# Equal operand offsets for large products, a rebuilt head with its own weight buffers, and a residual that is made later, in a hybrid SSD and sparse-attention block

## The chip, the core and the metric

The kernel runs on one core of a Trainium2 chip. The metric is the device time of one launch in microseconds (us). Engines are PE (TensorE: matmuls, and its weight loads PEld), DVE (VectorE), ACT (ScalarE), POOL (GpSimd) and SP (SyncE, which issues every DMA here).

## The reference, cut to what matters

One layer on `x` of 512 tokens by 1,024 channels, in float32, with one input LayerNorm ahead of it:

```python
h = _layernorm(x, ln_in_g, ln_in_b)
mix = _mixing(h, ...)                    # below
h = _layernorm(DN_ALPHA * h + mix, ln1_g, ln1_b)
f = _conv_ffn(h, ...)                    # w_up 1024 x 5632, conv over 3 tokens, silu(a) * v, w_down 2816 x 1024
h = _layernorm(DN_ALPHA * h + f, ln2_g, ln2_b)

def _mixing(h, w_in, ...):
    proj = h @ w_in
    z, xbc, dt, q, ckv, q_idx, k_idx, w_idx, g_ssd, g_att = jnp.split(proj, ...)
    y_ssd = _ssd_branch(z, xbc, dt, ..., D_skip, ...)        # y = scan(...) + xs * D_skip[:, None]
    y_att = _dsa_branch(q, ckv, q_idx, k_idx, w_idx, ...)    # 16 heads over a latent, top-128 keys
    m = jax.nn.sigmoid(g_ssd) * (y_ssd @ w_br_ssd) + jax.nn.sigmoid(g_att) * (y_att @ w_br_att)
    return m @ w_out
```

## The kernel before

All 512 tokens are worked at once. Activations that feed a product lie with channels on the 128 partitions (`hT`, `yT`, `mT`, `h1T`, `fT`), 512 tokens along a row of 2,048 bytes. Every large product is split: an operand `a` is kept as `hi`, a copy rounded to the type `fp32r`, and `lo = a - hi`, and a product is three matmuls, hi·hi, lo·hi and hi·lo, of 512 columns each (`mm3`, `tok_mm`). A weight arrives as a 512 KB tile `wraw` (`wload`), ACT rounds it into `whi` (L173), DVE subtracts into `wlo` (L174), and SP may load the next one into a `wraw` buffer when DVE has read it (two buffers, `bufs=2`).

The stages in order: the head (load `x`, LayerNorm, transpose, split into `hhi`/`hlo`; the products of `w_small` and the first two tiles of `w_qi`); the other projections of `h`; the SSD branch (`y`, tiles `yhi`/`ylo`) with `w_br_ssd`; attention head by head (`ya`), where `tm` on POOL (L763) is the mask plus the bias of one head; `w_br_att` (`m`); `w_out`; the first DeepNorm LayerNorm (`h1`); `w_up`, convolution and gate (`f`); `w_down`; the last LayerNorm.

Two pools take SBUF from two ends. Tiles of `wraw`, `whi`, `wlo`, `hhi`, `hlo`, `h1hi`, `h1lo`, the first 15 tiles `f` and the `wo` of three `w_out` steps come from the left end; the pool `wk`, with `y`, `ya`, `m`, the other 29 tiles of `f` (`fw`, `fx`, `fy`), the `wh` of the last weights of `w_out` and `w_down`, and the queries, keys and values, lies at the right end. All these tiles are multiples of 2,048 bytes long, so all of one end start at the same place modulo 2,048: 640 at the left end, 2,016 at the right end, and 1,696 for `ckhi`/`cklo`, which stand behind a 32-byte tile `m8`. Modulo 128 this is 0, 96 and 32.

In the head, `x` token tile 1 is normalized on ACT (L292, L293) and the others on DVE (L295). `last_pow` puts POOL's subtractions of the first two `wlo` (L303) behind POOL's last power for a reciprocal root (L155). POOL then makes the residual `h` in token layout, `x·g + b`, in 16 operations (L327, L328), each on a token tile's half, and SP stores it to `htok_d` (L330). It is loaded back as `h1` (L906) when `w_out`'s last weight is loaded, and read first by DVE at L914. The vector `D` is loaded by two DMAs of single elements (L482).

The order of the instructions on each engine is found at build time by a scheduler that works from priorities; `high_priority` and `issue_after` in the code move single ones.

Of the kernel before, what the change touches and what calls it, by code (L numbers as in the profile page):

```python
# [38 lines left out]
UNITS_B = [n / 18 for n in (1, 2, 2, 5)]  # L39
NOSYNC = mybir.DependencyInfo(mybir.DependencyClass.NoSync, mybir.DependencyReason.DATA)  # L40
# [3 lines left out]
ROWS = [("dt_bias", NH), ("A_log", NH), ("idx_g", 64), ("idx_b", 64)]  # L44
# [17 lines left out]

def half_of(h):
    return slice(h * T, (h + 1) * T)
# [3 lines left out]
def block_kernel(ctx, tc, A, out):  # L68
# [6 lines left out]
    wrw = E(tc.tile_pool(name="wrw", bufs=2))  # L75
    whl = E(tc.tile_pool(name="whl", bufs=3))
    dram = E(tc.tile_pool(name="dram", bufs=1, space=DRAM))
    ps_ = E(tc.tile_pool(name="ps", bufs=1, space=PSUM))
    wk = E(tc.tile_pool(name="wk", bufs=1, side="right"))
# [22 lines left out]
    def acc_tile():  # L102
        return ps("acc", 3)
# [18 lines left out]
    for i in range(NT):  # L122
        t = wt("k4" if i < 2 else "g4", [P, D], "x")
        nc.sync.dma_start(t, A["x"][tok(i)])
        xt.append(t)
    voff, vn = _offsets(VECS)
    pvec = ct([P, vn], "pvec")
    nc.sync.dma_start(pvec, A["pvec"])
    vec = {n: pvec[:, s] for n, s in voff.items()}

    ones = ct([P, P], "ones")
# [26 lines left out]
    def split(hi, lo, src):  # L158
        nc.scalar.activation(hi, src, AF.Copy)
        nc.vector.tensor_tensor(lo, src, hi.bitcast(F32), OP.subtract)  # L160
# [115 lines left out]
    m8 = kp.tile([P, 8], F32, name="m8")  # L276
# [4 lines left out]
    dt, dts, acT, cd = [kp.tile(SH, F32, name=n, tag=n) for n in ("dt", "dts", "acT", "cd")]  # L281


    raws = [wrw.tile([P, D], F32, name="wraw", tag="wraw") for _ in range(2)]
    nc.sync.dma_start(raws[0][:, :KD * 104], A["w_small"])
    nc.sync.dma_start(raws[1], A["w_qi"][0])
    stats = [ln_stats(t, i) for i, t in enumerate(xt)]
    for i, (t, (mv, rs)) in enumerate(zip(xt, stats)):
        if i == 1:
            nm = st([P, 1], "nm")  # L290
            nc.vector.tensor_scalar(nm, mv[:, 0:1], -1.0, None, OP.mult)
            nc.scalar.activation(t, t, AF.Identity, bias=nm)  # L292
            nc.scalar.activation(t, t, AF.Copy, scale=rs)  # L293
        else:
            nc.vector.tensor_scalar(t, t, mv[:, 0:1], rs, OP.subtract, OP.mult)  # L295
    wq = []
    for j, raw in enumerate(raws):
        hi = whl.tile([P, D], F32R, name="whi", tag="whi")
        lo = whl.tile([P, D], F32R, name="wlo", tag="wlo")
        cols = slice(0, D if j else KD * 104)  # L300
        nc.scalar.activation(hi[:, cols], raw[:, cols], AF.Copy)
        with tc.issue_after(last_pow[0].ins):
            nc.gpsimd.tensor_tensor(lo[:, cols], raw[:, cols], hi[:, cols].bitcast(F32), OP.subtract)  # L303
        wq.append((hi, lo))
    wq.append(w_("w_qi", 1, ahead=0))
    accs = [acc_tile() for _ in range(3)]
    trs = ["tr", "tr", "a", "b", "c", "tr", "tr", "a"]
    for k in range(KD):
# [9 lines left out]
        split(hhi[:, k], hlo[:, k], hf)  # L318


    for j in range(2):
        gB, bB = [wt("m2", [P, T], n) for n in ("gB", "bB")]
        nc.sync.dma_start(gB, bcast(A["ln_in_g"][half_of(j)], T))
        nc.sync.dma_start(bB, bcast(A["ln_in_b"][half_of(j)], T))
        for i in range(NT):
            xh = xt[i][:, half_of(j)]
            nc.gpsimd.tensor_tensor(xh, xh, gB, OP.mult)  # L327
            nc.gpsimd.tensor_tensor(xh, xh, bB, OP.add)  # L328
            if j == 1:
                nc.sync.dma_start(htok_d[:, i], xt[i])  # L330


    hTq = [(a[:, P:], b[:, P:]) for a, b in hT]
    TQ = T - P
# [771 lines left out]
```

## Time and profile before

| | |
|---|---|
| time, median of 3 runs | 1142.55 us (1140.33 to 1143.06) |
| profiled execution | 1140.93 us, span of its instructions 1139.2 us |
| mean granted TensorE clock | 0.994 of full speed |
| PE busy | 1104.3 us, 97% of the span |
| DVE, ACT, POOL busy | 806.7, 442.8, 184.3 us |

The span reaches from the first instruction to the last; 1.7 us of the execution lie around it. PE is busy nearly all the time from 40 us on, so an engine's busy time alone says little: what counts is when PE stands still and how far apart its matmuls start. A matmul's duration in the trace includes its way through the array, and the next one starts before it ends: the distance of two starts is the price of one.

### The profile page before, as it was taken

How to read it: one execution, taken by the hardware profiler on the slowest of the kernel's cores; microseconds unless marked ns; L12 is line 12 of the kernel's file. 1: busy time of each engine (PE TensorE's matmuls, PEld its weight loads, DVE VectorE, ACT ScalarE, POOL GpSimd, SP SyncE). 2: the span in 40 equal slices, each digit the busy share in tenths (PEclk: the TensorE clock that was granted, in tenths of full speed). 3: DMA queues.
4: the chain of work that ended last, by engine and by line, in shares of the span. 5: the costliest groups of instructions: out<-in, count | busy, mean ns of one | idle time of the engine just before them, and what ended most of it. 6: DMA issues, size and time to landing. Idle time of an engine off the chain costs nothing.

```text
span 1139.2 us, 14494 instructions
## 1 busy us (share of the span) xinstructions
PE 1104.3 (97%) x5394; PEld 902.7 (79%) x5394; DVE 806.7 (71%) x1536; ACT 442.8 (39%) x694; POOL 184.3 (16%) x179
## 2 busy tenths in 40 slices
PE   4799999999999999999999999999999999999996
PEld 3688888887888888878778778889888888888885
DVE  7479798876789899958998936586665566642227
ACT  3355344434333232335645523314444444432120
POOL 7600023312113122012323300040000000000002
PEclk9899999999999999999999999999999999999999
DMA  4452133363323322322211224622223222222241
GB/s 154 149 188 87 63 140 122 126 215 112 120 102 130 130 93 75 129 97 71 88 70 66 83 84 157 225 90 74 93 94 107 96 93 93 101 103 93 93 129 74
DMA packets 43718, 125.58 MB, mean 110 GB/s; under 512 B 6801, under 2 KB 11201, under 8 KB 43649
## 3 DMA queue, kind: packets, MB, share of 16 engines
q1 hardware_dynamic: 43648, 124.67, 31.4%
q8 instruction: 42, 0.69, 0.2%
q14 instruction: 28, 0.22, 0.1%
HBM read 118.20 MB, written 9.59 MB: 112 GB/s over the span
## 4 chain that ended last, share of the span: by engine, by line
PE 73%; DVE 2%; issue 0%; DMA 0%; ACT 0%; POOL 0%; DVEq 0%; SPq 0%; ACTq 0%; POOLq 0%
PE pacc L200 42%; PE pacc L224 5%; PE pc L200 5%; PE ptr L224 4%; PE pa L200 3%; PE pb L200 3%; PE pb L224 2%; PE pc L224 2%; PE pa L224 2%; PE ptr L200 2%; PE pb L203 1%; PE pc L580 1%; PE pa L203 1%; PE pb L576 0%; DMA G<-ac_d 0%
## 5 line engine op out<-in xcount | busy, mean ns | idle before, releaser
L174 DVE TENSOR_TENSOR wlo<-wraw,whi 128x1024 fp32r<-128x1024 f32 x161 | 205.2, 1275 | 165.6 <-ACT whi L173 165.2
L173 ACT ACTIVATE whi<-wraw 128x1024 fp32r<-128x1024 f32 x161 | 170.5, 1059 | 280.9 <-PE pacc L200 163.9
L200 PE MATMUL pacc<-hhi,whi 128*128 128x512 f32 (+1 forms) x552 | 223.7, 405 | 10.7 <-ACT whi L173 10.7
L200 PE MATMUL pacc<-hlo,whi 128*128 128x512 f32 (+2 forms) x552 | 217.2, 394 | 1.4 <-DVE hlo L160 1.4
L200 PE MATMUL pacc<-hhi,wlo 128*128 128x512 f32 (+2 forms) x552 | 215.8, 392 | 0.0
L200 PEld LDWEIGHTS pacc<-hhi,whi 128*128 128x128 f32 (+1 forms) x552 | 104.2, 189 | 33.6 <-ACT whi L173 11.2
L200 PEld LDWEIGHTS pacc<-hlo,whi 128*128 128x128 f32 (+1 forms) x552 | 104.1, 189 | 24.6 <-DVE hlo L160 2.2
L200 PEld LDWEIGHTS pacc<-hhi,wlo 128*128 128x128 f32 (+1 forms) x552 | 104.0, 189 | 18.1
L155 POOL TENSOR_TENSOR rs_y<-rs_v,mhalf 128x1 f32<-128x1 f32 (+1 forms) x18 | 17.1, 954 | 504.3 <-DVE rs_v L153 501.7
L200 PE MATMUL pacc<-h1hi,wlo 128*128 128x512 f32 (+1 forms) x216 | 79.0, 366 | 0.0
L200 PE MATMUL pacc<-h1hi,whi 128*128 128x512 f32 (+1 forms) x216 | 78.9, 366 | 0.0
L200 PE MATMUL pacc<-h1lo,whi 128*128 128x512 f32 (+1 forms) x216 | 78.7, 366 | 0.0
L763 POOL TENSOR_TENSOR tm<-mask,toe 128x128 f32<-128x128 f32 (+1 forms) x64 | 45.6, 715 | 166.2 <-DVE mn L774 102.7
L585 POOL TENSOR_TENSOR v<-v,eaB 128x384 f32<-128x384 f32 x16 | 23.7, 1483 | 238.1 <-DVE eaB L583 147.1
L497 DVE SCALAR_TENSOR_TENSOR cv<-pacc,cwb,cv 128x511 f32<-128x511 f32 (+2 forms) x72 | 53.3, 741 | 0.4
L200 PE MATMUL pacc<-yhi,whi 128*128 128x512 f32 x128 | 51.8, 406 | 0.1
L200 PE MATMUL pacc<-ylo,whi 128*128 128x512 f32 x128 | 51.1, 399 | 0.0
L200 PE MATMUL pacc<-yhi,wlo 128*128 128x512 f32 x128 | 50.6, 395 | 0.0
L777 ACT ACTIVATE l<-l,mn 128x128 f32<-128x128 f32 (+1 forms) x64 | 35.7, 559 | 33.5 <-DVE mn L774 31.9
L200 PEld LDWEIGHTS pacc<-h1hi,whi 128*128 128x128 f32 x216 | 40.7, 189 | 6.7
L200 PEld LDWEIGHTS pacc<-h1hi,wlo 128*128 128x128 f32 x216 | 40.8, 189 | 6.6
L200 PEld LDWEIGHTS pacc<-h1lo,whi 128*128 128x128 f32 x216 | 40.5, 188 | 6.5
(460 smaller groups left out, 2250.7 us busy)
## 6 DMA issues: line engine op xcount, KB each, us to landing
wraw<-in_w_up_dram SPq DMA_DIRECT2D x44, 512.0 KB, 3.4
wraw<-in_w_xbc_dram SPq DMA_DIRECT2D x24, 512.0 KB, 3.5
wraw<-in_w_down_dram SPq DMA_DIRECT2D x22, 512.0 KB, 3.4
G<-ac_d SPq DMA_DIRECT2D x16, 512.0 KB, 4.4
wraw<-in_w_z_dram SPq DMA_DIRECT2D x16, 512.0 KB, 3.5
wraw<-in_w_br_ssd_dram SPq DMA_DIRECT2D x16, 512.0 KB, 3.5
eaB<-ea_d SPq DMA_DIRECT2D x32, 128.0 KB, 3.2
wraw<-in_w_ga_dram SPq DMA_DIRECT2D x8, 512.0 KB, 3.5
```

The costliest lines, as they stand in the source:

```text
L155: last_pow[0] = nc.gpsimd.tensor_tensor(y, v, mhalf[:, :n], OP.pow)
L173: nc.scalar.activation(hi[:, :cols], raw[:, :cols], AF.Copy)
L174: nc.vector.tensor_tensor(lo[:, :cols], raw[:, :cols], hi[:, :cols].bitcast(F32), OP.subtract)
L200: pe(nc.tensor.matmul(p, a, b, start=start, stop=stop).ins)
L203: pe(nc.tensor.transpose(p, a, b).ins)
L224: nc.tensor.matmul(p, x[a][:, tok(i)], w[b][h], start=first and j == 0, stop=last and j == 2)
L497: nc.vector.scalar_tensor_tensor(y[:, d:], p[:, :T - d], cwb[:, 24 * k + c:24 * k + c + 1], y[:, d:], OP.mult, OP.add)
L580: nc.tensor.matmul(yd[h * 64:(h + 1) * 64, tok(c)], xd[:, c, h], G[:, h, c], start=True, stop=True)
L585: nc.gpsimd.tensor_tensor(v[:, P:], v[:, P:], eaB[:, P:], OP.add)
L763: nc.gpsimd.tensor_tensor(tm[:, :K - f], maskt[i][:, f:], self.toe[:, 2 * P - K + f:], OP.add)
L777: nc.scalar.activation(l[:, :K], l[:, :K], AF.Exp, bias=self.mn[:, ic], scale=-1.0, accum_out=self.sm[:, ic])
```

## The change

There are three parts.

**Offsets.** A pool `pad` of 352 bytes is placed at the right end ahead of `wk`, and `m8` moves behind `ckhi`/`cklo`. With the constants that the other edits add at the left, the tiles start at 832 modulo 2,048 at the left end, 1,664 at the right end and 1,856 for `ckhi`/`cklo`. Modulo 128 this is 64, 0 and 64; modulo 64 all are 0.

**Head.** The three first weights get `wraw` buffers of their own (`bufs=3`) and are loaded at once; the `whi`/`wlo` of both `w_qi` tiles lie in two `y8` tiles of the right end (`wq`). Their subtractions go from POOL to DVE, behind the last split of `h`. `x` tile 1 is normalized wholly on ACT (`center_act`). Normalized `x` is stored at once, without `g` and `b`. All products with the weights' `hi` come first, those with `lo` at the end. `D` comes with the row `prow`, and two small DVE copies make `Dv`.

**Residual.** The 16 POOL operations and their `g` and `b` move from the head to the end of the attention, where `x` is loaded from `htok_d` into the `h1` tiles.

```diff
+PAD = 88
@@ block_kernel
-    wrw = E(tc.tile_pool(name="wrw", bufs=2))
+    wrw = E(tc.tile_pool(name="wrw", bufs=3))
+    pad = E(tc.tile_pool(name="pad", bufs=1, side="right"))
+    pad.tile([P, PAD], F32, name="pad")
     wk = E(tc.tile_pool(name="wk", bufs=1, side="right"))
@@ head
+    raws = [wrw.tile([P, D], F32, name="wraw", tag="wraw") for _ in range(3)]
+    nc.sync.dma_start(raws[0][:, :KD * 104], A["w_small"])
     nc.sync.dma_start(pvec, A["pvec"])
+    for j in range(2):
+        nc.sync.dma_start(raws[1 + j], A["w_qi"][j])
+    prow = wt("m2", [P, rn], "prow")
+    nc.sync.dma_start(prow, bcast(A["prow"], rn))
...
-    stats = [ln_stats(t, i) for i, t in enumerate(xt)]
-    for i, (t, (mv, rs)) in enumerate(zip(xt, stats)):
+    def center_act(t):
+        s, q = st([P, 1], "act_s"), st([P, 1], "act_q")
+        nc.scalar.activation(t, t, AF.Identity, accum_out=s)
+        nc.vector.tensor_scalar(s, s, -1.0 / D, None, OP.mult)
+        nc.scalar.activation(t, t, AF.Identity, bias=s)
+        for j in range(2):
+            sq = wt("v", [P, T], "sqj")
+            nc.scalar.activation(sq, t[:, half_of(j)], AF.Square, accum_out=q if j == 0 else s)
+        nc.vector.tensor_tensor(q, q, s, OP.add)
+        return rsqrt_small(q, 1.0 / D, EPS, 1, 1)
+    for i, t in enumerate(xt):
         if i == 1:
-            nc.scalar.activation(t, t, AF.Identity, bias=nm)
-            nc.scalar.activation(t, t, AF.Copy, scale=rs)
+            rs = center_act(t)
+            scaled = nc.scalar.activation(t, t, AF.Copy, scale=rs)
         else:
+            mv, rs = ln_stats(t, i)
             nc.vector.tensor_scalar(t, t, mv[:, 0:1], rs, OP.subtract, OP.mult)
-        with tc.issue_after(last_pow[0].ins):
-            nc.gpsimd.tensor_tensor(lo[:, cols], raw[:, cols], hi[:, cols].bitcast(F32), OP.subtract)
-    wq.append(w_("w_qi", 1, ahead=0))
+        nc.sync.dma_start(htok_d[:, i], t)
+    y8s = [flat(wt("y8", [P, 4, T], "wq", F32R)) for _ in range(2)]
+    wq += [[y[:, half_of2(j)] for y in y8s] for j in range(2)]
...
+        last = split(hhi[:, k], hlo[:, k], hf)
+    with tc.issue_after(last.ins):
+        for w, raw, cols in zip(wq, raws, wcols):
+            nc.vector.tensor_tensor(w[1][:, cols], raw[:, cols], w[0][:, cols].bitcast(F32), OP.subtract)
-            nc.gpsimd.tensor_tensor(xh, xh, gB, OP.mult)
-            nc.gpsimd.tensor_tensor(xh, xh, bB, OP.add)
-                nc.sync.dma_start(htok_d[:, i], xt[i])
     for k in range(KD):
-        mm3(accs[0][:104], wq[0], slice(k * 104, (k + 1) * 104), hT[k], k == 0, k == KD - 1)
+        for p, w, m, r in first:
+            for x_ in r[k]:
+                mm(p, w[0][:, k * m:(k + 1) * m], x_, start=k == 0 and x_ is r[k][0], stop=False)
+    for p, w, m, r in first:
+        for k in range(KD):
+            mm(p, w[1][:, k * m:(k + 1) * m], r[k][0], start=False, stop=k == KD - 1)
+    for b in range(2):
+        hs = slice(b * 64, (b + 1) * 64)
+        nc.vector.tensor_copy(Dv[hs], row["D"][hs].rearrange("p (q b) -> p b q", b=2)[:, b])
-        nc.sync.dma_start(Dv[b * 64:(b + 1) * 64],
-                          bass.AP(tensor=Da.tensor, offset=Da.offset + b, ap=[[0, 64], [2, NH // 2]]))
@@ behind the attention
+    h1 = [wt("k4" if i < 2 else "g4", [P, D], "h1") for i in range(NT)]
+    with tc.issue_after(last_w[0].ins):
+        for (n, j), t in lir.items():
+            nc.sync.dma_start(t, bcast(A["ln_in_" + n][half_of(j)], T))
+        for i in range(NT):
+            nc.sync.dma_start(h1[i], htok_d[:, i])
+    for i in range(NT):
+        for j in range(2):
+            t = h1[i][:, half_of(j)]
+            nc.gpsimd.tensor_tensor(t, t, lir["g", j], OP.mult)
+            nc.gpsimd.tensor_tensor(t, t, lir["b", j], OP.add)
@@ at w_out
-        for i in range(NT):
-            nc.sync.dma_start(h1[i], htok_d[:, i])
```

SP's queue at the program's start, before the change:

```order
L124 DMA x<-in_x_dram 128x1024 x4
L128 DMA pvec<-in_pvec_dram 128x346
L285 DMA wraw<-in_w_small_dram 128x832
L286 DMA wraw<-in_w_qi_dram 128x1024
L323 DMA gB<-in_ln_in_g_dram 128x512
L324 DMA bB<-in_ln_in_b_dram 128x512
L323 DMA gB<-in_ln_in_g_dram 128x512
L324 DMA bB<-in_ln_in_b_dram 128x512
L342 DMA prow<-in_prow_dram 128x192
L482 DMA Dv<-in_ssd_D_dram 64x16x1 x2
L167 DMA wraw<-in_w_qi_dram 128x1024 x3
L167 DMA wraw<-in_w_ckv_dram 128x1024 x2
```

And SP's queue at the same place after it:

```order
L132 DMA x<-in_x_dram 128x1024 x4
L135 DMA wraw<-in_w_small_dram 128x832
L138 DMA pvec<-in_pvec_dram 128x346
L141 DMA wraw<-in_w_qi_dram 128x1024 x2
L144 DMA prow<-in_prow_dram 128x224
L322 DMA htok_d<-x 128x1024 x4
L184 DMA wraw<-in_w_qi_dram 128x1024 x2
L184 DMA wraw<-in_w_ckv_dram 128x1024 x2
```

The second `w_qi` tile no longer stands behind the two loads of `Dv` nor behind a buffer; the stores of `x` stand between it and the third tile.

DVE's queue in the head after the change, from the scaling of `x` tiles 2 and 3 to the first weights that come by `wload` (`hf` is a transposed and scaled piece of `h`):

```order
L321 TENSOR_SCALAR x<-x,ln_mv_179,rs_y_3_183 128x1024
L361 COPY Dv<-prow 64x16 x2
L345 TENSOR_SCALAR hf<-ptr,pvec 128x512
L345 TENSOR_SCALAR hf<-pa,pvec 128x512
L177 TENSOR_TENSOR hlo<-hf,hhi 128x512
L345 TENSOR_SCALAR hf<-pc,pvec 128x512
L177 TENSOR_TENSOR hlo<-hf,hhi 128x512 x2
L345 TENSOR_SCALAR hf<-ptr,pvec 128x512
L177 TENSOR_TENSOR hlo<-hf,hhi 128x512
L345 TENSOR_SCALAR hf<-pa,pvec 128x512
L177 TENSOR_TENSOR hlo<-hf,hhi 128x512 x4
L349 TENSOR_TENSOR wlo<-wraw,whi 128x832
```

The three `wlo` of the head (L349; two of them write `wq`) stand at the end of the eight splits `hlo`; before the change two of them were on POOL.

POOL's queue at the end of the attention, before the change, with the `tm` of the last head and what follows them:

```order
L763 TENSOR_TENSOR tm<-mask_112,toe 128x128
L763 TENSOR_TENSOR tm<-mask_113,toe 128x256
L763 TENSOR_TENSOR tm<-mask_114,toe 128x256
L763 TENSOR_TENSOR tm<-mask_115,toe 128x256
L155 TENSOR_TENSOR rs_y_0_6631<-rs_v_0_6629,mhalf 128x1
```

And after it (`h_6120` to `h_6123` are the four token tiles of `h1`):

```order
L887 TENSOR_TENSOR h_6120<-h_6120,lig 128x512
L887 TENSOR_TENSOR h_6122<-h_6122,lig 128x512
L888 TENSOR_TENSOR h_6120<-h_6120,lib 128x512
L775 TENSOR_TENSOR tm<-mask_125,toe 128x128
L775 TENSOR_TENSOR tm<-mask_126,toe 128x256
L888 TENSOR_TENSOR h_6122<-h_6122,lib 128x512
L775 TENSOR_TENSOR tm<-mask_127,toe 128x256
L775 TENSOR_TENSOR tm<-mask_128,toe 128x256
L887 TENSOR_TENSOR h_6121<-h_6121,lig 128x512
L888 TENSOR_TENSOR h_6121<-h_6121,lib 128x512
```

Three residual operations now stand ahead of the last head's first `tm`, and one between its second and third.

## Rows read from the trace of the kernel before

**Rows 1.** The page's first part: busy time of each engine in us, its share of the span, instructions.

```profile
PE 1104.3 (97%) x5394; PEld 902.7 (79%) x5394; DVE 806.7 (71%) x1536; ACT 442.8 (39%) x694; POOL 184.3 (16%) x179
```

**Rows 2.** Busy time by stretch of the span: us from and to, width, then PE, PEld, DVE, ACT and POOL busy us (x instructions), the granted TensorE clock as a share of full speed, DMA share, GB/s.

```profile
25.80:36.50 10.70, 0.10 (x1) 0.00 (x0) 1.71 (x2) 1.01 (x2) 10.70 (x9) 0.67 0.27 98
36.50:40.00 3.50, 3.40 (x10) 2.92 (x11) 3.42 (x3) 1.60 (x4) 3.50 (x3) 0.55 0.17 34
```

**Rows 3.** The timeline of the first 50 us, all engines: start us, duration us, engine, line, operation, out<-in, shape, count, and in brackets the idle time before it and what ended it.

```profile
5.68 1.28 ACT L292 ACT_TABLE_LOAD   x1 [5.68 <-DMA x<-in_x_dram]
...
9.75 1.85 SPq L482 DMA_DIRECT2D Dv<-in_ssd_D_dram  x2
...
10.70 1.15 ACT L293 ACTIVATE x<-x,rs_y 128x1024 f32<-128x1024 f32 x1
...
12.79 2.17 POOL L303 TENSOR_TENSOR wlo<-wraw,whi 128x832 fp32r<-128x832 f32 x1
...
14.98 23.64 SPq L167 DMA_DIRECT2D wraw<-in_w_qi_dram  x3
...
15.56 0.69 PE L311 MATMUL ptr<-ident,x 128*128 128x128 f32 x2 [1.02 <-DVE x L295]
...
16.08 0.81 DVE L317 TENSOR_SCALAR hf<-ptr,pvec 128x512 f32<-128x512 f32 x1 [0.57 <-PE ptr L311]
...
16.94 1.97 PE L311 MATMUL ptr<-ident,x 128*128 128x128 f32 x8
...
19.28 0.48 PE L200 MATMUL pacc<-hhi,whi 128*104 128x512 f32 x1
...
20.37 0.62 ACT L159 ACTIVATE hhi<-hf 128x512 fp32r<-128x512 f32 x1
...
22.82 0.40 PE L200 MATMUL pacc<-hhi,whi 128*104 128x512 f32 x1
...
23.05 0.57 PE L200 MATMUL pacc<-hhi,wlo 128*104 128x512 f32 x2
...
35.49 1.06 ACT L173 ACTIVATE whi<-wraw 128x1024 fp32r<-128x1024 f32 x1 [14.49 <-DMA wraw<-in_w_qi_dram]
...
36.60 0.69 PE L200 MATMUL pacc<-hhi,whi 128*128 128x384 f32 x1 [10.70 <-ACT whi L173]
...
37.51 0.63 PE L200 MATMUL pacc<-hhi,whi 128*104 128x512 f32 x1
```

**Rows 4.** The same timeline, PE alone, where the first three accumulators end: the last product into them and the first into `pb`.

```profile
47.35 0.33 PE L200 MATMUL pacc<-hlo,whi 128*128 128x384 f32 x1
47.52 0.34 PE L200 MATMUL pb<-hhi,whi 128*128 128x384 f32 x1
```

**Rows 5.** DMA issues of the first 60 us: out<-in, queue, operation, count, KB each, median us from issue to landing.

```profile
Dv<-in_ssd_D_dram SPq DMA_DIRECT2D x2, 4.0 KB, 18.7
```

**Rows 6.** Groups of instructions over the whole span, shapes apart: line, engine, operation, names, shape, count | busy us, mean ns of one | idle us before them and what ended it.

```profile
L174 DVE TENSOR_TENSOR wlo<-wraw,whi 128x1024 fp32r<-128x1024 f32 x161 | 205.2, 1275 | 165.6 <-ACT whi L173 165.2
...
L200 PE MATMUL pacc<-h1hi,whi 128*128 128x512 f32 x168 | 65.4, 389 | 0.0
...
L224 PE MATMUL pacc<-whi,fw 128*128 128x512 f32 x48 | 15.6, 396 | 0.0
...
L327 POOL TENSOR_TENSOR x<-x,gB 128x512 f32<-128x512 f32 x8 | 11.8, 1493 | 0.0
...
L160 DVE TENSOR_TENSOR hlo<-hf,hhi 128x512 fp32r<-128x512 f32 x8 | 11.0, 1408 | 0.0
...
L160 DVE TENSOR_TENSOR ylo<-v,yhi 128x512 fp32r<-128x512 f32 x16 | 10.2, 683 | 0.0
...
L200 PE MATMUL pacc<-cklo,whi 128*128 128x512 f32 x16 | 6.3, 396 | 0.0
```

**Rows 7.** The chain that ended last, in order of time: start us, us, engine, tile, line, number of instructions in the piece. The first row lies where `y`·w_br_ssd and `h` products alternate, the second in the w_br_att stage.

```profile
457.82 40.36 PE pacc L200 x175
...
678.70 41.67 PE pacc L200 x178
```

**Rows 8.** The same chain, its last stretch alone (w_down), same columns.

```profile
1044.80 2.04 PE pacc L224 x9
...
1050.33 2.09 PE pacc L224 x9
...
1106.53 2.11 PE pacc L224 x9
1108.64 5.45 PE ptr L224 x24
```

**Rows 9.** POOL's timeline behind the attention's end, columns as in rows 3.

```profile
647.43 1.28 POOL L763 TENSOR_TENSOR tm<-mask,toe 128x128 f32<-128x128 f32 x2 [1.95 <-DVE mn L774]
...
743.17 1.00 POOL L155 TENSOR_TENSOR rs_y<-rs_v,mhalf 128x1 f32<-128x1 f32 x1 [89.39 <-DVE rs_v L153]
```

**Rows 10.** PE's timeline: the last matmul that reads head 13's queries and keys. Columns as in rows 3.

```profile
641.93 0.39 PE L200 MATMUL ptr<-Kl,Q 128*128 128x512 f32 x1
```

**Rows 11.** DVE's timeline: the first use of head 15's `tm`, and the first use of the residual.

```profile
656.26 0.29 DVE L774 CUSTOM_DVE_ANT_0 l<-ptr,tm 128x128 f32<-128x128 f32 x1 [0.42 <-PE pa L203]
...
737.46 0.69 DVE L914 SCALAR_TENSOR_TENSOR h<-h,ptr 128x512 f32<-128x512 f32 x1 [2.68 <-PE ptr L224]
```

**Rows 12.** Busy time by stretch, columns as in rows 2: the stretch behind the attention.

```profile
665.00:682.00 17.00, 16.64 (x76) 12.01 (x77) 3.58 (x7) 1.96 (x4) 0.00 (x0) 1.00 0.18 62
```

## Prediction before the run

> **What bounds the kernel now.** I read the page's first part first: PE is busy 97% of the span [rows 1]. So a gain must come from one of two places: time in which PE stands still, or matmuls that start too far apart. The table by stretch shows where PE stands still: from 25.8 to 36.5 us it works for 0.10 of 10.70 us, and in the 3.5 us behind that its granted clock is 0.55 of full speed, so for most of them the lower of its two levels (1.2 against 2.4 GHz), after a stretch without matmuls [rows 2]. The distances between starts are the second place: the pieces of the chain that ended last, with their counts, give them below.
>
> **The head, before.** PE's first product starts at 19.28, 3.72 us behind the first transposes of the last `x` tile (15.56), and the first product into the next accumulator `pb` at 47.52 [rows 3, 4]. In these 28.2 us lie 72 products. A 512-column one costs 0.23 us (22.82 to 23.05) and a 384-column one 0.17 us [rows 3, 4], so 24 × 0.23 + 48 × 0.17 = 13.7 us of work: 14.5 us are lost. Most is one stall of 10.70 us that waits for `whi` [rows 3]. ACT makes it at 35.49, after 14.49 us of waiting for the second `w_qi` tile, and three `hhi` stand behind it on ACT. That load was issued at 14.98, behind the two loads of `Dv` (9.75) [rows 3]; `Dv`, 4 KB each, needs a median of 18.7 us to land [rows 5]. The buffer it needed had been held until then by POOL's subtraction of the first `wlo` (12.79, 2.17 us) [rows 3]. Matmuls at the lower clock (0.63 us long at 37.51, 0.40 at 22.82) and waits for `hlo`, which takes 1408 ns beside POOL's work where the same operation takes 683 ns elsewhere [rows 3, 6], make up the rest.
>
> **The head, after.** Nothing of `Dv` is left in front of the loads, and three buffers let all first weights load at once. What decides then is the chain of `x` tile 1, which goes wholly over ACT and comes last. It lands by 5.68 (ACT's first operation waits for it) [rows 3]. Two passes of 1.15 us, two half passes of 0.62 [rows 3] and, estimated, 0.2 for reading out each sum and 0.7 for DVE's factor between them end near 10.4. Adding the sums on DVE, behind the statistics of `x` tile 3, and the power, last of four in POOL's order at about 1.0 each [rows 9], need until about 13.4; the scaling ends near 14.6. 27 transposes follow (eight in 1.97 us with the way through the array [rows 3], so 0.21 each), which PE finishes near 20.3; `hf` costs 0.81 and `hhi` 0.62 [rows 3], so PE's first product stands at 19.5 to 20.4. From there 13.7 us of products without a wait end near 33.8. DVE must keep up: eight splits at 683 ns [rows 6] and five `hf` at 0.81 from 16.5 on end near 26; the three `wlo` (1275 ns for 1,024 columns [rows 6]) are ready at 27.2, 28.5 and 29.7. PE comes to them at 29.3, 31.1 and 32.4, so this move costs nothing while POOL is quiet; with DVE at the 1408 ns of before it would cost about 4 us. The third `w_qi` tile is loaded when the first `wlo` frees its buffer (27.2) and split by 33.3, just in time. The stores of `x` (2 MB, now at 10 to 15 us) lie beside a stretch in which PE still transposes. The sum: 47.5 − 33.8 = 13.7 us, less about 0.7 for a clock that may be low after the idle 4 us ahead of `x` tile 1. I take **13.0**, between 9 (DVE late, clock low) and 14.5 (all that is lost).
>
> **The offsets.** Equal pairs and unequal ones run at two fixed rates. In w_down the chain goes over from one to the other in one loop: 9 matmuls take 2.04 us (226.7 ns each) while `f` lies at the left like `whi`, and 2.09 to 2.11 (232 to 234) from 1050.33 on, when `f` lies at the right [rows 8]. The last four weights lie at the right too and cost 227 (5.45 for 24) [rows 8]; they start at 2,016, so it isn't alignment itself but the difference that counts. In w_br_att 178 matmuls take 41.67 us: 234.1 [rows 7]. So an unequal product costs 7.4 ns more. By the code: `y` 384, `ya` 192, w_out 120, w_down 248 and `ck` 96 are unequal, 1,040 × 7.4 = 7.7 us. Where equal and unequal ones alternate the mean lies halfway (457.82: 175 in 40.36, 230.6) [rows 7], as it should. A difference of 32 (`cklo,whi`) and one of 96 (`whi,fw`) cost the same, 396 ns in mean against 389 for the equal `h1hi,whi` [rows 6], which speaks for a modulus of 64, and by that all pairs become equal. But left to right is then 64 modulo 128, and no row of before shows such a pair. From below: if 128 is the modulus, only `ck` gains (0.7) and 48 products of the head lose (0.3): 0.4. I take equality modulo 64 as the likelier, at 0.7, and of its 7.7 I count **6.3**: a stream needs some matmuls after each interruption to fall into the faster rate, and where PE waits for something else in between, nothing is won.
>
> The Trainium skill (SBUF — State Buffer, "SBUF: two separate sides") says that the ports of PE never wait on anyone; by it an offset could change nothing, this term would be 0 and the sum 1128.4. The two rates in one loop speak against it, but not for the modulus.
>
> **The residual.** 16 POOL operations (1493 ns each [rows 6] beside DVE, so 22 to 24 us) leave the head, where they also doubled `hlo`, and come to the attention's end. POOL is idle there for 89.39 us up to 743.17, and the first use of the residual is at 737.46 [rows 9, 11]. Three of them stand ahead of the last head's first `tm`. Their tile is free when head 13's keys were last read (641.93 [rows 10]); load and landing take 4 to 5 us, three operations 4.5: `tm` is ready near 651 instead of 648, and first needed at 656.26 [rows 11]: 5 us to spare. The other 12 lie about 665 to 682, where DVE works for 3.58 of 17 us [rows 12], so a DVE operation that waits for POOL is late by one or two us at most, and `whi`/`wlo` are three deep. The loads move away from w_up's. **+0.5**, between −0.5 and +2; without the cover of idle POOL it would be all of 22.
>
> **The sum**, against the profiled execution: 1140.93 − 13.0 − 6.3 + 0.5 = 1122.1. The median of the runs lies 1.6 above that execution; I add about half of it and forecast **1123**. The scheduler may reorder the middle for ±2. Its own range is 1118 to 1127.
>
> **Rivals.**
> - *The offsets don't do what the change says* (equality would have to be modulo 128, or PE doesn't care and the rates have another cause): the term is 0.4, 1140.93 − 13.0 − 0.4 + 0.5 = 1128, with the same 0.9 on top 1129. For it: no pair at 64 was ever run. Against: 32 and 96 cost the same. 0.25. The skill's sentence on the ports would end here too.
> - *The head's gain is cut*: `x` tile 1 late, the clock at its lower level for the first products, or DVE late for `wlo`. Gain 8 instead of 13: 1128; with the first rival 1134. For it: ten operations of three engines now lie in a row ahead of the first product. Against: each has a row, and the sum leaves 2 us at each `wlo`. 0.10.
> - *Slower*: the residual's operations on POOL stand ahead of the last head's `tm`. If the second tile's load landed late, `tm` and with it softmax, transposes and products of the last head wait, and `w_br_att` behind them. It costs from a landing of 10 us on, and the kernel is slower than before only if it takes all 19 us and 3.4 more, a landing near 32 us. Against: loads of that size land within a few us there. Result 1146 or more. 0.03.
> - The rest, 0.07: small orders of the scheduler and of the DMA queues that come out better or worse by 5 us.
>
> **How the numbers follow.** The likeliest (all three parts as priced) has 0.55. To hold 8 in 10 the range takes in the first rival and the better half of the second: 1116 to 1131, with the lower end where head and offsets give all they can (14.5 and 7.7, and no cost of the residual: 1118.7) and the scheduler 2 more. About 0.3% (3.4 us) can be told from no change; below 1139.1 end all cases but the slow one and a heap of mishaps: faster 0.94, same 0.03, slower 0.03.
>
> **What would show it.** Right: no idle time of PE above 2 us between the first product and `pb`, and `pb` near 34 us; in w_br_att and in the second half of w_down 24 matmuls in 5.44 us (24 × 226.7); POOL busy between 655 and 685, and PE there no less than now. Wrong: 24 in 5.6 us there (the first rival); `pb` behind 38, or a granted clock near 0.5 behind 15 us (the second); `ptr` or `pacc` waiting for DVE's `mn` or for POOL's `tm` between 650 and 665 (the third).

## The result and the profile after

| | before | after |
|---|---|---|
| median | 1141.88 us (4 runs, 1140.33 to 1143.06) | 1128.80 us (4 runs, 1128.65 to 1129.35) |
| profiled execution, span | 1140.93, 1139.2 us | 1128.71, 1127.0 us |

The ratio is 0.989, with an interval of 0.9878 to 0.9902. The change makes the kernel 13.1 us faster, where the prediction had 19. The time lies inside the range of 1116 to 1131, and 0.2 us from the 1129 of the first rival; but it comes about differently from either case, as the stages show.

The first and second part of the page of the changed kernel. PE is now busy 98% of its span, against 97% [rows 1]; POOL has lost 9 us of work, and the granted clock is under 90% in the third slice alone, from 56 to 85 us:

```profile
PE 1099.4 (98%) x5394; PEld 903.2 (80%) x5394; DVE 803.6 (71%) x1538; ACT 443.2 (39%) x701; POOL 175.4 (16%) x177
...
PEclk9989999999999999999999999999999999999999
```

**The head.** The timeline of the changed kernel (start, duration, engine, operation, and in brackets the idle time ahead with its releaser):

```profile
14.18 1.54 PE L339 MATMUL ptr<-ident,x 128*128 128x128 f32 x6 [5.15 <-ACT x L318]
...
18.53 0.47 PE L217 MATMUL pacc<-hhi,whi 128*104 128x512 f32 x1
...
24.21 1.02 DVE L349 TENSOR_TENSOR wlo<-wraw,whi 128x832 fp32r<-128x832 f32 x1
...
25.15 2.35 DVE L349 TENSOR_TENSOR wq<-wraw,wq 128x1024 fp32r<-128x1024 f32 x2
...
29.07 1.06 ACT L190 ACTIVATE whi<-wraw 128x1024 fp32r<-128x1024 f32 x1 [6.52 <-DMA wraw<-in_w_qi_dram]
...
32.58 0.33 PE L217 MATMUL pb<-hhi,whi 128*128 128x384 f32 x1
```

The chain of `x` tile 1 ends, as foreseen, as the last: its transposes wait for ACT until 14.18. The first product starts at 18.53 and `pb` at 32.58, where it started at 47.52 [rows 4]; no bracket stands at either. The three `wlo` are ready at 25.2 and 27.5, and the third `w_qi` tile is split at 30.13, so the 6.5 us that ACT waits for it are covered. The head gains 47.52 − 32.58 = 14.9 us in this profile. In the profiles of the eight kernels below that keep this head (e1_pad40 to e8_nores), `pb` starts at 33.23 to 34.15, so it gains 13.4 to 14.3 there. From the groups by form, DVE in the first 40 us (count, then busy us and mean ns): `hlo` is back at the duration that the same operation had elsewhere, half of the 1408 ns of before [rows 6]:

```profile
L177 DVE TENSOR_TENSOR hlo<-hf,hhi 128x512 fp32r<-128x512 f32 x8 | 5.1, 684 | 0.0
```

**Behind the head.** What PE waits for in the changed kernel (total us, times, longest):

```profile
PE pacc L217 <- DVE cv L509: 2.0, 1, 2.0
PE pa L259 <- ACT cks L478: 1.6, 1, 1.6
PE pc L217 <- DVE pt L805: 0.7, 1, 0.7
...
PE pc L465 <- DVE acT L463: 0.5, 1, 0.5
```

None of these four stands among PE's waits in the kernel before. Two of them lie at 60 to 62 us, in the stretch behind the head where the decays and the latents are made. PE's timeline there:

```profile
57.48 1.06 PE L454 MATMUL pc<-upper,sp 128*32 128x128 f32 x8
...
60.28 0.46 PE L465 MATMUL pc<-acT,lastrow 128*128 128x128 f32 x2 [0.48 <-DVE acT L463]
62.29 0.59 PE L259 MATMUL pa<-ones,cks 128*128 128x1 f32 x2 [1.56 <-ACT cks L478]
...
63.31 0.63 PE L217 MATMUL pacc<-hhi,wlo 128*128 128x512 f32 x1
63.74 0.63 PE L217 MATMUL pacc<-hlo,whi 128*128 128x512 f32 x1
...
68.41 0.40 PE L217 MATMUL pacc<-hhi,wlo 128*128 128x512 f32 x1
68.64 0.40 PE L217 MATMUL pacc<-hlo,whi 128*128 128x512 f32 x1
```

The windows of the changed kernel around 60 and 165 us (length; busy us of PE, PEld, DVE, ACT, POOL; granted clock, DMA share, GB/s):

```profile
60.00:70.00 10.00, 8.17 (x27) 6.55 (x27) 7.64 (x24) 5.83 (x10) 0.00 (x0) 0.66 0.63 216
165.00:180.00 15.00, 13.01 (x85) 10.62 (x84) 14.31 (x33) 7.25 (x10) 3.78 (x3) 0.92 0.43 150
```

From 57.48 to 62.74 PE gets small matmuls with three products and two waits between. Behind them 13 products start 0.43 us apart (63.31 to 63.74) instead of 0.23 (68.41 to 68.64): the lower of the two clock levels, 13 × 0.2 = 2.6 us beside the 2.0 us of waiting. Two things differ from the kernel before. PE arrives 13 us earlier (57.48 against 70.43). And the scheduler has found another order: before, twelve products (71.42 to 74.41) stood between the first small matmuls of this stage and the next ones, and now there are three. On ACT, `cks` started 2.3 us behind those first small matmuls, and now it starts 4.2 us behind them (61.76), after `whi`, `cv` and `ear`. Which of the two it is that makes the waits is taken up with the last experiments.

The other wait, 1.99 us ahead of a product at 177.26, is for a `cv` (L509) that stands on DVE behind work on `G` from 172.71 on; DVE is busy 14.31 of the 15 us around it, and the clock is 0.92 there.

**The offsets.** The chain that ended last (start, length, and how many matmuls): in w_br_att 178 take 40.96 us, 230.1 ns each, where they took 41.67 [rows 7]. In w_down nine take 2.10 us still, as before [rows 8]:

```profile
667.58 40.96 PE pacc L217 x178
...
1094.37 2.10 PE pacc L241 x9
```

So w_br_att gained 0.7 us where the working had 178 × 7.4 ns = 1.3, and w_down nothing: there the rate of before, with operands 96 bytes apart modulo 256, and the one of now, with 64, read the same.

**The residual.** POOL's timeline at the attention's end:

```profile
633.93 2.72 POOL L887 TENSOR_TENSOR h<-h,lig 128x512 f32<-128x512 f32 x2 [1.24 <-DMA h<-htok_d]
```

And PE's:

```profile
640.97 2.37 PE L217 MATMUL pc<-pt,V 128*64 128x512 f32 x14 [0.71 <-DVE pt L805]
```

Four of the 16 operations run from 633.93 to 641.64, with two `tm` at 638.83 between them; PE waits 0.71 us behind. The last of the 16 end at 688, long before the first use. What the move costs in all is measured below.

### The profile page after: what moved, and what is told of

The parts are those of the page before. It is cut to its first block, busy times and chain, and to the rows that moved or that the text cites. A ratio compares the mean times of both kernels' runs of the same rounds, so it can differ in the third digit from the quotient of the medians.

```text
span 1127.0 us, 14500 instructions
## 1 busy us (share of the span) xinstructions
PE 1099.4 (98%) x5394; PEld 903.2 (80%) x5394; DVE 803.6 (71%) x1538; ACT 443.2 (39%) x701; POOL 175.4 (16%) x177
## 4 chain that ended last, share of the span: by engine, by line
PE 95%; DVE 2%; DMA 1%; issue 0%; ACT 0%; POOL 0%; SPq 0%; DVEq 0%; ACTq 0%; POOLq 0%
PE pacc L217 58%; PE pc L217 6%; PE pacc L241 5%; PE ptr L241 4%; PE pa L217 3%; PE pb L217 3%; PE pb L241 2%; PE pa L241 2%; PE pc L241 2%; PE ptr L217 2%; PE pc L592 1%; PE pb L588 1%; PE pa L569 1%; PE pb L220 1%; PE pa L220 1%; PE ptr L558 1%
## 5 line engine op out<-in xcount | busy, mean ns | idle before, releaser
L217 PE MATMUL pacc<-hhi,whi 128*128 128x512 f32 (+1 forms) x536 | 219.5, 410 | 2.0 <-DVE cv L509 2.0
L217 PE MATMUL pacc<-hlo,whi 128*128 128x512 f32 (+1 forms) x536 | 213.0, 397 | 0.0
L217 PE MATMUL pacc<-hhi,wlo 128*128 128x512 f32 (+1 forms) x536 | 211.1, 396 | 0.0
L217 PEld LDWEIGHTS pacc<-hhi,whi 128*128 128x128 f32 (+1 forms) x536 | 101.9, 190 | 24.5 <-issue 3.9
L217 PEld LDWEIGHTS pacc<-hlo,whi 128*128 128x128 f32 (+1 forms) x536 | 101.5, 189 | 22.3 <-issue 1.2
L509 DVE SCALAR_TENSOR_TENSOR cv<-pacc,cwb,cv 128x511 f32<-128x511 f32 (+2 forms) x72 | 53.3, 741 | 0.5
```

What stands on the lines that cost most here:

```text
L217: pe(nc.tensor.matmul(p, a, b, start=start, stop=stop).ins)
L509: nc.vector.scalar_tensor_tensor(y[:, d:], p[:, :T - d], cwb[:, 24 * k + c:24 * k + c + 1], y[:, d:], OP.mult, OP.add)
```

## Experiments

All times are medians, with the ratio to the kernel before on the same chip. "Apart" below is the distance of the operands' starts modulo 256 bytes, left end against right end, worked out from the lengths of the tiles.

### What distance the offsets need

Four kernels change the one number `PAD`, and with it the starts at the right end:

```diff
-PAD = 88
+PAD = 40      # e1_pad40: 0 apart (1,024 bytes)
+PAD = 8       # e2_pad8: 128 apart
+PAD = 0       # e3_pad0: 160 apart, the part on offsets undone
+PAD = 104     # e5_pad104: 0 apart (768 bytes)
```

> The changed kernel with PAD 40 for 88 and nothing else: the right end starts at 1,856 modulo 2,048, so right and left (832) differ by 1,024, which is 0 modulo 512. The order of instructions is the same. Theory A (a pair is equal only if the difference is 0 modulo a number above 64): all large products run at 226.7 ns, w_down at 2.04 us for 9 matmuls throughout, w_br_att at 5.44 us for 24; against the changed kernel's 1128.8 that is about 1,000 products by 3 to 6 ns, so 1123 to 1126. Theory B (the ports of PE never wait on anyone, offsets do nothing): 1128.8 within 1 us, w_down 2.10 for 9.

> The changed kernel with PAD 8: right and left differ by 1,152, which is 0 modulo 128, but 128 modulo 256 and modulo 512. Same order of instructions. If the number is 128: the same gain as with PAD 40, 1123 to 1126, 226.7 ns per product. If it is 256 or 512: rates like those of the changed kernel (229 to 234 ns), 1127 to 1130. Theory B: 1128.8 within 1 us.

> The changed kernel without the pad: right and left differ by 1,184, 32 modulo 64, much as before the change; the ck tiles stay equal to the left end. This undoes the offset part alone. If the step from 32 to 64 modulo 128 gave what the two traces show (w_br_att 41.67 to 40.96 us for 178 matmuls, w_down 2.11 to 2.10 for 9, the y products alike): 2 to 3.5 us slower than the changed kernel, 1131 to 1132. Theory B: 1128.8 within 1 us.

> The changed kernel with PAD 104: right and left differ by 768, which is 0 modulo 256 and 256 modulo 512. Same order of instructions. With PAD 40 (0 modulo 512) all products ran at 226.7 ns, with PAD 8 (128 modulo 256) w_br_att needed 41.65 us for 178 and w_down 2.10 for 9. If the number is 256: as PAD 40, 2.04 and some 40.6, and 1123 to 1126. If it is 512: as PAD 8, 2.10 and above 40.9, and 1128 to 1130.

The chain that ended last, w_br_att and (of the first three) one step of the second half of w_down, of the four in that order:

```profile
666.50 40.57 PE pacc L217 x178
...
1046.89 2.04 PE pacc L241 x9
```
```profile
668.02 41.65 PE pacc L217 x178
...
1067.37 2.10 PE pacc L241 x9
```
```profile
670.55 41.83 PE pacc L218 x178
...
1048.10 2.10 PE pacc L242 x9
```
```profile
667.21 40.57 PE pacc L217 x178
```

The last column but one is the time from the first of these 178 products to the end of the span, which lies behind all the waits that are treated below. The four came out as expected for a modulus of 256, e3_pad0 0.4 us above its range.

| kernel | apart | 178 products of w_br_att | from there to the end | median, ratio |
|---|---|---|---|---|
| e1_pad40 | 0 | 40.57 us | 456.5 us | 1125.12, 0.9853 [0.9837, 0.9869] |
| e5_pad104 | 0 | 40.57 us | 456.5 us | 1125.53, 0.9857 [0.9843, 0.9872] |
| the change | 64 | 40.96 us | 459.4 us | 1128.80, 0.9890 [0.9878, 0.9902] |
| e2_pad8 | 128 | 41.65 us | 459.9 us | 1129.23, 0.9893 [0.9878, 0.9907] |
| e3_pad0 | 160 | 41.83 us | 460.6 us | 1132.43, 0.9917 [0.9902, 0.9931] |
| before | 96 | 41.67 us [rows 7] | 460.5 us | 1141.88 |

Equality modulo 64 or 128 doesn't give the fast rate, since e2_pad8 has both and runs at 234 ns. Equality modulo 512 isn't needed, since e5_pad104 (768 bytes) runs like e1_pad40. So it is modulo 256 that counts, of the distances that were tried. The change's 64 lies between the two rates in w_br_att and at the slow one in w_down. One thing differs between these two loops: in w_br_att the weight at the left end is the operand that PE holds (PEld loads it) and `ya` from the right end streams through, while in w_down `f` from the right end is held and the weight streams. Streaming minus held is then +64 in the one and −64, or 192 modulo 256, in the other. The rows fit a rate that goes by this signed distance; no kernel tested it.

Undoing the part costs 1132.43 − 1128.80 = 3.6 us by the medians. By stretches it is somewhat more. The profile of e3_pad0 loses 1.7 us against the change's between `pb` and the SSD branch at 253 us, with the same clock of 0.66 at 60 us; 1.6 in the SSD branch; and 1.1 from w_br_att on. That is 4.4, and its attention is 1.0 us shorter for a reason of its own (below). To come from 64 bytes to 0 gives 3.0 us from w_br_att on and 0.6 in the SSD branch, and the medians say the same: 3.7 and 3.3 us to e1_pad40 and e5_pad104. In these two stretches alone, equal operands are thus worth 6.2 us against a distance of 160 bytes.

The whole spans are no clean measure, because the clock behind the stall at 60 us isn't the same in all profiles: the windows from 60 to 70 us of e1_pad40, e2_pad8 and e5_pad104 have 0.83, those of the change and of e3_pad0 0.66, which is worth some 1.7 us (0.17 of 10 us). Of the 3.2 us between e2_pad8 and e3_pad0, 1.5 lie in the two stretches above.

### What the wait at 60 us costs

The first trial puts the sum over the squares behind the first products of `w_xbc`:

```diff
             nc.scalar.activation(cks[j], p, AF.Square)
-        rb = rms_bcast(cks, 256)
+        yield
+        with tc.issue_after(last_pe[0]):
+            rb = rms_bcast(cks, 256)
...
+    lat = latents()
+    next(lat)
     scores()
...
+    in0 = ssd_in(0)
+    next(in0)
+    next(lat, None)
```

> The changed kernel, with the mean-square matmuls of the latents (L259, which wait for the squares cks from ACT) traced behind the first products of w_xbc on PE instead of ahead of them. My theory: the new stall of PE at 61 us (1.56 us waiting for cks) and the half granted clock behind it (0.65 from 60 to 70 us) vanish: 4 to 4.5 us faster than the changed kernel, 1124.5. Rival: PE waits at the next small matmul instead (L465, or the first use of cv), and the clock falls all the same: 1127 to 1129.

Measured: 1131.12 us, 0.9903 [0.9887, 0.992], so not faster than the change, and outside of what both the theory and its rival had. The longest of PE's waits behind the head in this kernel:

```profile
PE pa L571 <- DVE xdd L566: 2.3, 1, 2.3
...
PE pacc L217 <- ACT cks L478: 1.1, 1, 1.1
```

The wait for `cks` is still there, now at an accumulator that ACT hasn't read out, and waits of 2.3 and 1.5 us for DVE have come later. Moving the waiting matmul did not help. The next trial takes work from ACT: the squares are made on DVE from `ck`, and PE comes to the sum 24 products later. It was run with the change's pad and with e1_pad40's:

```diff
             nc.scalar.activation(ck[j], p, AF.Copy)
-            nc.scalar.activation(cks[j], p, AF.Square)
+            nc.vector.tensor_tensor(cks[j], ck[j], ck[j], OP.mult)
```

> The changed kernel, but the squares cks of the latents are made by DVE from the copy ck instead of by ACT from PSUM. The scheduler then sets the small matmuls (L462, L259) 24 products later on PE. My theory: the stall at 61 us (0.5 + 1.6) and the half granted clock behind it go, without a new wait: 1124 to 1125. Rival (as in the run that moved the matmuls alone): PE is early for the ACT and DVE work of this stage as a whole, the waits come back behind it, 1128 or more.

> The same with PAD 40. If the two effects add: the time of PAD 40 (1125.1) less what the squares on DVE give, 1120 to 1122, faster than both kernels. If the stall comes back elsewhere: 1125.

Measured: 1122.74 us, 0.9837 [0.982, 0.9854], and 1120.52 us, 0.9811 [0.9797, 0.9826]. The windows of the first:

```profile
60.00:70.00 10.00, 10.00 (x56) 8.31 (x56) 7.81 (x22) 4.74 (x7) 0.00 (x0) 1.00 0.47 178
165.00:180.00 15.00, 15.00 (x90) 11.81 (x89) 15.00 (x33) 7.12 (x10) 4.72 (x3) 1.00 0.45 155
```

Both stretches are full, at the whole clock: the waits at 60 and, though nothing was changed near it, at 177 us are gone, and no wait of PE behind the head is longer than 0.7 us. One edit of two instructions, with the order that the scheduler makes of it, gives 1128.80 − 1122.74 = 6.1 us, more than the 4.0 us of waiting that it removes. The low clock behind the waits is the rest: 20 products take 6.42 us behind the wait at 177 us in the change, against 4.9 in e1_pad40, which has the same wait and a clock of 1.00 there. The gain is larger than the 4 to 5 us of the theory.

The second kernel is the fastest of all, 8.3 us below the change. The two parts don't quite add: at PAD 40 the squares on DVE give 1125.12 − 1120.52 = 4.6 us (5.0 from e5_pad104), at PAD 88 6.1. Its window shows a lower clock although PE is never idle in it:

```profile
60.00:70.00 10.00, 10.00 (x51) 8.28 (x50) 8.39 (x24) 4.05 (x7) 0.00 (x0) 0.89 0.50 174
```

Eight products are 0.43 us apart there, from 67.92 to 71.40, right behind 2.2 us of short matmuls. e6_dvecks88 has the same order and a clock of 1.00. So the low stretch doesn't need a wait, and it doesn't come each time.

### What the residual costs

```diff
-            nc.gpsimd.tensor_tensor(t, t, lir["g", j], OP.mult)
-            nc.gpsimd.tensor_tensor(t, t, lir["b", j], OP.add)
+            if j == 0:
+                nc.gpsimd.tensor_tensor(t[:, :8], t[:, :8], lir["g", j][:, :8], OP.mult)
+                nc.gpsimd.tensor_tensor(t[:, :8], t[:, :8], lir["b", j][:, :8], OP.add)
```

> The changed kernel without most of the residual's g and b: the 16 POOL operations at the end of the attention are left out but for 8 small ones on 8 columns each, so that the loads, waits and places stay. Theory (hidden behind idle POOL, +0.5): 1128.8 less 0 to 0.8. Rival (they delay the last head's tm or DVE's operations): 3 us or more faster, with less waiting of PE between 640 and 690 us.

Measured: 1126.30 us, 0.9859 [0.9843, 0.9875], so 2.5 us faster than the change, between what the theory and its rival had. The chain of the changed kernel from the end of the SSD branch to w_br_att, then that of e8_nores, then that of the kernel before:

```profile
508.80 4.81 PE pacc L217 x21
...
667.58 40.96 PE pacc L217 x178
```
```profile
508.30 4.81 PE pacc L217 x21
...
665.31 40.96 PE pacc L217 x178
```
```profile
521.57 4.80 PE pacc L200 x21
```

Up to there the two profiles are 0.5 us apart. Attention takes 158.8 us in the change, 157.0 without the residual and 157.1 before (to 678.70 [rows 7]), and from w_br_att on the first two take 459.4 and 459.5. So POOL's work costs 1.8 us. All of it lies at the 16 products with `V` around 640 us, which take 4.1 us (from 639.18) against 2.3 (from 638.69): more than the 0.7 us for which PE is idle behind them. DVE's work ahead of them fits that, in the change and without the residual:

```profile
635.37 2.36 DVE L191 TENSOR_TENSOR wlo<-wraw,whi 128x1024 fp32r<-128x1024 f32 x1
```
```profile
634.88 1.22 DVE L191 TENSOR_TENSOR wlo<-wraw,whi 128x1024 fp32r<-128x1024 f32 x1
```

One `wlo` and the operation behind it (`mssd`, 1.77 against 0.69 us) take about twice as long beside POOL's residual, and the `pt` that PE waits for comes after them. In e3_pad0 POOL begins a little later, this `wlo` takes 1.22 us, and attention is 1.0 us shorter than in the change.

### What the head owes to `Dv` and to the third buffer

Each of the two is made alone in the kernel before: in the first `D` comes with `prow`, as in the change; in the second the pool of raw weights has three buffers.

```diff
-        nc.sync.dma_start(Dv[b * 64:(b + 1) * 64],
-                          bass.AP(tensor=Da.tensor, offset=Da.offset + b, ap=[[0, 64], [2, NH // 2]]))
+        hs = slice(b * 64, (b + 1) * 64)
+        nc.vector.tensor_copy(Dv[hs], row["D"][hs].rearrange("p (q b) -> p b q", b=2)[:, b])
```
```diff
-    wrw = E(tc.tile_pool(name="wrw", bufs=2))
+    wrw = E(tc.tile_pool(name="wrw", bufs=3))
```

> The kernel before the change, with one edit: D comes with the row prow and two small DVE copies make Dv, so its two loads of single elements are gone; two wraw buffers, POOL's subtractions and the residual in the head stay. Theory A (Dv's elements held the second w_qi tile up on the DMA rings): its load, issued at 15, lands near 20 instead of 35.5, PE's stall of 10.7 us falls below 2, 9 to 11 us faster: 1131 to 1133. Theory B (the shared buffer, or POOL's load, is what holds the head up): the load lands early but POOL's subtraction and the slow hlo keep PE waiting, less than 5 us gained, above 1137.

> The kernel before the change, with one edit: three wraw buffers for two, so that both w_qi tiles are loaded ahead of Dv. Theory A: the stall moves to the third w_qi tile, whose load now stands behind Dv: PE waits near 33 us for a whi that comes at 36, so 6 to 9 us are gained: 1133 to 1136. Theory B (the buffer was the cause): 10 us or more gained, no stall behind it.

Measured: 1134.65 us, 0.9942 [0.9927, 0.9956], and 1133.93 us, 0.9934 [0.9916, 0.9952]. Of the first, PE's longest wait behind the first product:

```profile
PE pacc L200 <- DVE hlo L160: 3.2, 1, 3.2
```

`hlo` in it, by form:

```profile
L160 DVE TENSOR_TENSOR hlo<-hf,hhi 128x512 fp32r<-128x512 f32 x8 | 12.3, 1582 | 0.0
```

And the load of `w_qi` (KB each, median us from issue to landing):

```profile
wraw<-in_w_qi_dram SPq DMA_DIRECT2D x4, 512.0 KB, 3.4
```

Without the loads of `Dv` a `w_qi` tile lands in a median of 3.4 us; in the kernel before it took 12.4. The 10.7-us stall is gone, and `pb` starts at 39.26, 8.3 us earlier. A wait of 3.2 us for `hlo` has taken the place of a part of it, because POOL's residual still runs beside DVE. The time lies between the two theories, with the stall gone as the first had it and a gain of 7.2 us, where it had 9 to 11. Of the second kernel, `pb`'s first matmul:

```profile
37.34 0.45 PE L200 MATMUL pb<-hhi,whi 128*128 128x384 f32 x1 [1.06 <-ACT whi L173]
```

And the load of `w_qi`:

```profile
wraw<-in_w_qi_dram SPq DMA_DIRECT2D x4, 512.0 KB, 13.8
```

Here the loads are as slow as before, but start earlier, and `pb` stands at 37.34, 10.2 us earlier, as the first theory had it. Either edit alone gives 7 to 8 us, and added up the two would be more than the 14.5 us that the head had lost: each is enough to remove the long stall. The other parts of the head were not undone one by one. The other way round, the changed kernel with the two loads of elements put back behind `prow`:

```diff
+        nc.sync.dma_start(Dv[b * 64:(b + 1) * 64],
+                          bass.AP(tensor=Da.tensor, offset=Da.offset + b, ap=[[0, 64], [2, NH // 2]]))
...
-    nc.vector.tensor_copy(Dv[hs], row["D"][hs].rearrange("p (q b) -> p b q", b=2)[:, b])
```

> The changed kernel with Dv loaded by the two DMAs of single elements again, issued behind prow. Theory A: they occupy the rings until about 30 us, the third w_qi tile (issued at 25) lands some 4 us later than 29 and PE waits 1 to 4 us at 33: 1130 to 1133. Theory B (own buffers are enough): 1128.8 within 1 us.

Measured: 1139.45 us, 0.9983 [0.9973, 0.9992]; its profile, of 1144.16 us, is the slowest of its executions. `pb`'s first matmul in it:

```profile
41.29 0.69 PE L221 MATMUL pb<-hhi,whi 128*128 128x384 f32 x1 [7.58 <-ACT whi L194]
```

The loads and stores of its first 60 us:

```profile
htok_d<-x SPq DMA_DIRECT2D x4, 512.0 KB, 22.8
...
Dv<-in_ssd_D_dram SPq DMA_DIRECT2D x2, 4.0 KB, 20.4
```

Two loads of 4 KB take back 10.6 of the change's 13.1 us, far above the 1 to 4 that the theory had. The third buffer and the moved subtractions don't protect from them, because all that is issued behind them on that queue is late: the stores of `x` land after 22.8 us and the third `w_qi` tile so late that PE waits 7.58 us.

These three kernels also tell what makes the waits at 60 us. e9_b_dv and e10_b_buf keep the order of the kernel before in that stage, and PE reaches it 8 us earlier than before, at 62.44 and 62.50 (in the change 13 us earlier). In e9_b_dv:

```profile
62.44 1.06 PE L436 MATMUL pc<-upper,sp 128*32 128x128 f32 x8
...
66.77 0.38 PE L242 MATMUL pa<-ones,cks 128*128 128x1 f32 x2
```

Neither of the two has a wait there, and the clock from 60 to 85 us is 1.00. e11_a_dv has the order of the change, and reaches the stage at 69.13, nearly as late as the kernel before:

```profile
69.13 1.06 PE L455 MATMUL pc<-upper,sp 128*32 128x128 f32 x8
...
71.92 0.46 PE L466 MATMUL pc<-acT,lastrow 128*128 128x128 f32 x2 [0.47 <-DVE acT L464]
73.94 0.59 PE L263 MATMUL pa<-ones,cks 128*128 128x1 f32 x2 [1.56 <-ACT cks L479]
```

It has the same waits of 0.47 and 1.56 us, and the one of 2.0 for `cv`. So they go with the scheduler's new order, and not with the early arrival of PE.

## Why the prediction came out as it did

**The head: right.** Forecast 13.0 us between 9 and 14.5, measured 14.9 in the change's profile and 13.4 to 14.3 in eight others with the same head, so that about one of the 1.9 us above the term is scatter of a single profile. The mechanism was the one in the working: `x` tile 1 last, the products with `wlo` behind it without a wait. The first product stood at 18.53 instead of 19.5 to 20.4 (at 19.13 to 20.11 in the eight others), and the `wlo` were ready two us earlier than worked out. The deduction for a low clock wasn't needed: the 72 products took 14.05 us (18.53 to 32.58), against 13.7 by the full rates.

**The offsets: the step that failed is the modulus.** The prediction read 396 ns for differences of both 32 and 96 bytes, took that to speak for 64, and gave it 0.7. But the 396 at 32 was no sign of a slow distance. In the change the starts of `cklo` and `whi` are 1,024 bytes apart, equal modulo 256, and the mean is much the same:

```profile
L217 PE MATMUL pacc<-cklo,whi 128*128 128x512 f32 x16 | 6.3, 394 | 0.0
```

So one slow distance was read, 96, and one can't tell 64 from 128 or 256; the working itself had said that no row showed the change's own distance. The size was nearly right for operands that are equal as PE counts it: 6.2 us in the SSD branch and from w_br_att on alone and 6.9 to 7.3 by the medians of e3_pad0 against e1_pad40 and e5_pad104, where the working had 6.3, and 7.7 before its deduction. The change reached 3.6 to 4.4, with w_br_att at a rate between the two and w_down at the slow one. So neither the 6.3 of the forecast nor the 0.4 of the rival came true. The Trainium skill (SBUF — State Buffer, "SBUF: two separate sides") says that PE's ports never wait on anyone; the loops at 2.04 and 2.10 us, with nothing but `PAD` changed between the kernels, show that the start addresses of PE's own operands change its rate all the same.

**A new wait behind the head: missing.** The prediction looked for a wait that takes the place of the old one only up to `pb`, and for the rest counted on "±2 for the scheduler". The scheduler's new order for the stage at 60 us cost more than that: the waits of 0.5, 1.6 and 2.0 us and the low clock after them cost 6.1 us by the medians, which e6_dvecks88 gives back. That it is the order is shown by e9_b_dv, e10_b_buf and e11_a_dv; which instruction the scheduler should have placed otherwise is not. This is a loss of the size of "the head's gain is cut", but at a place and by a mechanism that the second rival didn't name.

**The residual: the place was right, the size was not.** Forecast +0.5 between −0.5 and +2, measured 1.8, within the range but above the term. The operations ahead of the last head's `tm` were the place, as described. But the working gave `tm` 5 us to spare and looked for late DVE operations only behind 665 us; the cost came at 635 to 639 us, where DVE's own operations take about twice as long beside POOL, as `hlo` had in the head. The third rival (1146) is out: the loads landed in time.

Added up by the stretches of the two profiles, the change gains 14.9 us up to `pb`, loses 2.2 from there to the end of the SSD branch (508.80 − 32.58 against 521.57 − 47.52), loses 1.7 in attention and gains 1.1 from w_br_att on: the 12.2 us between the spans. In the stretch that loses 2.2 the offsets give 3.3 (1.7 and 1.6, taken from e3_pad0), so the waits and the low clock cost about 5.5 there. The terms of the forecast therefore came out as 14.9 for 13.0, 4.4 for 6.3, a loss of 5.5 to 6.1 for which there was no term, and a loss of 1.8 for 0.5. That the time lies inside the range, next to the 1129 of the first rival, is luck: the range was widened for a case that did not happen, and what filled it was a loss that nobody had named.

Of the signs named ahead, `pb` near 34 and no wait above 2 us came; 24 products in 5.44 us in w_br_att did not (40.96 × 24 / 178 = 5.52), which shows by itself, without an experiment, that the offsets were not equal as the engine counts it.

## What to carry to other kernels

An edit in one place can change the order that a scheduler finds in another, and a wait of 2 us at a place with only short matmuls can cost the critical engine more than that, with the clock that falls behind it. To learn whether a new wait comes from the order or from an earlier arrival, look at kernels that have the one without the other. A rate that depends on an address is measured at the very distance that the change produces: a slow row says nothing on which other distances are fast, and one run with another pad is cheap. Loads of single elements don't belong on the queue in front of the first weights; a row that comes in with others, and two small copies, do the same.

## What was not expected of the hardware

- Products of type fp32r with 512 columns start 226.7 (nine in 2.04 us) to 227.9 ns apart when the two operands' starts are equal modulo 256 bytes, and 230 to 235 at distances of 64, 96, 128 and 160 (178 in 40.57 us at 0; 40.96, 41.67, 41.65 and 41.83 at the others).
- Two DMAs of 4 KB, made of single elements, take 18.7 to 20.4 us to land and hold back what is issued behind them on the queue: a 512 KB load needs 11.5 to 13.8 us instead of 3.4, and a store 22.8.
- Behind a wait of 1.6 us and some short matmuls the granted clock stayed at the lower level for some 5 us. In other kernels with the same wait the window's clock was 0.83 instead of 0.66, so the price of one stall differs by some 1.7 us between profiles. Behind the short matmuls alone, without a wait, it was 0.89 in one kernel and 1.00 in another.
- DVE operations on two tiles take about twice as long while POOL works on the residual: `wlo` 2.36 us against 1.22, `hlo` 1408 and 1582 ns against 684.
